# Gate and branch projections of a hybrid block: from weights on the stationary side with 256 tokens moving, to token tiles on the stationary side with 512 weight columns moving

## The chip, the cores and the metric

The kernel runs on one core of one Trainium2 chip. The metric is the device time of one execution in microseconds (us). TensorE (PE) does the matrix products, VectorE (DVE) and ScalarE (ACT) the elementwise work, GpSimd (POOL) mostly issues small transfers, and SyncE (SP) issues the weight loads. Engines run independently and wait for one another on semaphores; a tile in a rotating pool can be written again only when its last reader is done.

## The reference

One layer, one sequence of 256 tokens, width D = 2048, all in fp32:

```
mod = silu(c) @ w_ada + b_ada ;  sh1, sc1, g1, sh2, sc2, g2 = split(mod, 6)
h = rms_norm(x, mix_norm_pre) * (1 + sc1) + sh1
ya, yb, yc = hgrn2(h @ w_in ...), dilated_attention(...), conv_module(...)
gates = sigmoid(h @ w_gate + b_gate).reshape(B, S, 3, D)
merged = gates[0] * (ya @ w_a_out) + gates[1] * (yb @ w_b_out) + gates[2] * (yc @ w_c_out)
x = x + g1 * rms_norm(merged @ w_o, mix_norm_post)
h = rms_norm(x, mlp_norm_pre) * (1 + sc2) + sh2
x = x + g2 * rms_norm(square(relu(h @ w_up)) @ w_down, mlp_norm_post)
```

The change concerns `gates`, the three branch projections (2048 of their input columns together) and `merged`, which the product with `w_o` reads.

## The kernel before

Every product of two fp32 matrices is made of three products of split values. A weight tile `raw` of 512 KB is loaded by SP, ACT casts it to its high part `hi` (L126), DVE subtracts to get the low part `lo` (L127), and PE adds up weight-hi by activation-hi, weight-hi by activation-lo and weight-lo by activation-hi.

The work is one list of **jobs**, written out in Python in the order in which the weights are to be used. A job is one 512 KB load, its split, its matmuls, and what has to be done when its output tile is complete. `run` (L176) walks the list: up to five loads are issued ahead of the job at hand and up to four splits are made ahead; there are six `raw`, six `hi` and six `lo` tiles. So SP's queue holds the weight loads in list order, and each engine sees the instructions in the order in which the walk wrote them.

The jobs the change touches are the 96 **gate jobs** (12 gate tiles `g` of 512 output columns, for four column groups n and three branches b, eight jobs each) and the 32 **projection jobs** (four groups n, eight jobs: four for branch 0, one for branch 1, three for branch 2). The first 32 gate jobs stand by themselves. The others are woven with the projection jobs, the first `w_o` jobs and 96 **ada jobs** (names `wada`, `adap`, `adat`): such a job loads 512 KB too, but has no matmul: DVE multiplies the tile by the broadcast condition and sums along it (L297). In the stretch of gates there is nearly one ada job for each gate job. After every eighth ada job of the first 32, POOL writes 2 KB to a scratch in DRAM in elements of 4 bytes (L841, `np_scratch`) and reads it back repeated to all partitions (L843).

Both gate and projection jobs call `mm_a`: for each of two 128-row slices of the weight tile and each of four groups of 128 weight columns, the weights are the stationary operand and the 256 tokens move, 24 matmuls with 256 columns each. Outputs stand with weight columns on partitions, tokens along the tile. That makes the gate's bias one number per partition, which ACT adds while it reads the gate's sums out of PSUM (L824, four instructions of 256 elements). The finished `merged[n]` is already in the layout that the `w_o` product needs, so it is only split (L879 on ACT, L880 on DVE). The `w_o` jobs already use `mm_b`, in which a tile of 128 tokens is the stationary operand and 512 weight columns move, 12 matmuls for a job; so do the jobs of the first input projections (names L264 to L266; L252 to L254 belong to `mm_a`).

Of the kernel before, what the change touches and what calls it, by code (L numbers as in the profile page):

```python
# [19 lines left out]
P = 128  # L20
# [25 lines left out]
VEC = {}  # L46
_o = 0
for _n, _w in (("c", 16), ("lb", 8), ("b1", 32), ("b2", 32), ("bg1", 16), ("bg2", 16),
               ("n1", 16), ("n2", 16), ("np1", 16), ("np2", 16), ("bg", 48), ("cw", 186), ("cb", 6), ("lng", 6), ("lnb", 6),
               ("hw", 1)):  # L50
    VEC[_n] = (_o, _o + _w)
    _o += _w
# [4 lines left out]
def hybrid_block(ctx: ExitStack, tc: tile.TileContext, a, out, dbg=None):  # L57
# [182 lines left out]
    def mm_a(ps, h, l, na, ah, al, first, last, tk=None):  # L240

        t0, t1 = (0, S) if tk is None else (tk * P, (tk + 1) * P)
        bk = ps if isinstance(ps, list) else [ps[:, 0, :], ps[:, 1, :]]
        head = first and tk != 1
        for i in range(na):
            f, e = head and i == 0, last and i == na - 1
            x, y = ah[i][:, t0:t1], al[i][:, t0:t1]
            for j in range(h.shape[2] // P):
                o = bk[j // 2][:, (j % 2) * S + t0:(j % 2) * S + t1]
                w = slice(j * P, (j + 1) * P)  # L250
                b0, b1 = j % 2 == 0, j % 2 == 1
                nc.tensor.matmul(o, h[:, i, w], x, start=f and b0, stop=False, skip_group_check=True)  # L252
                nc.tensor.matmul(o, h[:, i, w], y, start=False, stop=False, skip_group_check=True)  # L253
                nc.tensor.matmul(o, l[:, i, w], x, start=False, stop=e and b1, skip_group_check=True)  # L254
# [13 lines left out]
    def ps_unit():  # L268
        return psg.tile([P, 2, 512], F32, tag="g", name=nm("g"))
# [120 lines left out]
    def h_hi(kt):  # L390
        return hT[kt // 2][:, 0, kt % 2, :]

    def h_lo(kt):
        return hT[kt // 2][:, 1, kt % 2, :]
# [417 lines left out]
    st_ln = []  # L812

    def gate_job(b, n, ch):
        def fn(h, l):
            if ch == 0:
                pst["gt"] = ps_unit()
            kts = [2 * ch, 2 * ch + 1]
            mm_a(pst["gt"], h, l, 2, [h_hi(k) for k in kts], [h_lo(k) for k in kts], ch == 0, ch == 7)
            if ch == 7:  # L820
                gates[b, n] = s4([P, 4, S])
                for j in range(4):
                    c = b * 16 + n * 4 + j
                    g = nc.scalar.activation(gates[b, n][:, j, :], pst["gt"][:, j // 2, (j % 2) * S:(j % 2 + 1) * S],  # L824
                                             AF.Sigmoid, bias=V("bg")[:, c:c + 1])
                if (b, n) == (2, 3):
                    with tc.issue_after(g.ins):
                        st_ln.append(nc.scalar.preload_act_table_set("natural_log_exp_and_others"))
        return Job(a["wg"][(b * 4 + n) * 8 + ch], [P, 2, 512], fn, budget=B_G)

# [21 lines left out]
    def act_of(ki):  # L852
# [3 lines left out]
            return ybT[0]  # L856
        return ycT[ki - 5]

    def proj_job(n, ki):
        b = 0 if ki < 4 else (1 if ki == 4 else 2)  # L860
        first, last = ki in (0, 4, 5), ki in (3, 4, 7)

        def fn(h, l):
            if first:
                pst["pj"] = ps_unit()
            t = act_of(ki)
            mm_a(pst["pj"], h, l, 2, [t[:, 0, 0, :], t[:, 0, 1, :]], [t[:, 1, 0, :], t[:, 1, 1, :]], first, last)
            if last:
                g = gates[b, n]
                gv = g.rearrange("p a b -> p (a b)")  # L870
                nc.vector.tensor_mul(gv, pst["pj"].rearrange("p a b -> p (a b)"), gv)
                if b == 0:
                    merged[n] = g
                else:
                    nc.vector.tensor_add(merged[n], merged[n], g)
                if b == 2:
                    mh = s4([P, 4, S], F32R)
                    ml = s4([P, 4, S], F32R)
                    nc.scalar.copy(mh, merged[n])  # L879
                    nc.vector.tensor_sub(ml, merged[n], mh.bitcast(F32))  # L880
                    mhl[n] = (mh, ml)
                    dump(f"mg{n}", merged[n].rearrange("p a b -> p (a b)"))
        return Job(a["wp"][n * 8 + ki], [P, 2, 512], fn, budget=B_P)

# [309 lines left out]
def layout(inputs):  # L1194
# [16 lines left out]
    for k in range(3):  # L1211
# [13 lines left out]
    ad = cat(pair(sc1, sh1) + [g1] + pair(sc2, sh2) + [g2], 1)  # L1225
    a["wada"] = np.ascontiguousarray(ad.T.reshape(96, P, 2, 1024).transpose(0, 2, 1, 3)).reshape(192, P, 1024)
    a["wada0"] = _chunks(cat([sc1[:, :256], sh1[:, :256]], 1))
    b = i["b_ada"][0].reshape(6, D)
    two = lambda u, v: np.ascontiguousarray(np.stack([_cols(u, 16), _cols(v, 16)], 2)).reshape(P, 32)
    cw = i["conv_w"][0].T.reshape(6, P, 31).transpose(1, 0, 2).reshape(P, 186)  # L1230
    a["vec"] = np.ascontiguousarray(cat([
        _cols(i["c"], 16), _cols(i["hgrn_lb_logits"], 8), two(b[1], b[0]), two(b[4], b[3]), _cols(b[2], 16),
        _cols(b[5], 16), _cols(i["mix_norm_pre"], 16), _cols(i["mlp_norm_pre"], 16), _cols(i["mix_norm_post"], 16),
        _cols(i["mlp_norm_post"], 16), _cols(i["b_gate"], 48), cw,
        _cols(i["conv_b"], 6), _cols(i["conv_ln_g"], 6), _cols(i["conv_ln_b"], 6), _cols(i["hgrn_norm_w"], 1)], 1))
    return a

# [13 lines left out]
```

## Time and profile before

| quantity | value |
|---|---|
| time, median of 3 runs | 1692.66 us (1688.83 to 1697.15) |
| time of the profiled execution | 1685.17 us |
| its span, first to last instruction | 1683.1 us |
| mean granted clock of TensorE | 0.995 of full speed |
| PE busy | 1631.5 us, 97% of the span |
| DVE busy | 1163.8 us, 69% |
| ACT busy | 748.1 us, 44% |
| POOL busy | 48.7 us, 3% |
| DMA, mean over the span | 240 GB/s |

The profile is of one execution; 2.1 us of its time lie outside the span. Busy times are shares of the whole span, over stages that differ much: the gate and projection jobs lie between about 310 and 850 us, and what holds there has to be read from views of that stretch. A matmul's busy time overlaps with that of the next, so the distance from one start to the next, and not the duration of a row, is what a matmul takes in a stream.

### The profile page before, as it was taken

The numbers are of one execution on the slowest core, as the hardware profiler recorded it, in microseconds if no ns is written. First come the engines' busy times: TensorE is split into PE (matmuls) and PEld (weight loads), VectorE is DVE, ScalarE is ACT, GpSimd is POOL, SyncE is SP. The second block draws the span as 40 slices with busy tenths as digits, with TensorE's granted clock in tenths as the row PEclk, the third lists the DMA queues.
The fourth block names the chain that finished last, engine by engine and source line by source line (L and its number), as shares of the span: only waits on it lengthen the run. The fifth ranks groups of instructions, "written<-read, shape, count | busy, mean of one in ns | idle before, by whom it ended". The sixth has DMA issues, their size and how long they took to land.

```text
span 1683.1 us, 27691 instructions
## 1 busy us (share of the span) xinstructions
PE 1631.5 (97%) x11142; PEld 1507.7 (90%) x11142; DVE 1163.8 (69%) x1549; ACT 748.1 (44%) x891; POOL 48.7 (3%) x74
## 2 busy tenths in 40 slices
PE   5999999989999999999999899999999999999997
PEld 3899999877999999999988799999999988888886
DVE  5899979638898986898896665454545745444444
ACT  3644443334453453444444654434444644333333
POOL 0000000110000000000000300000000000000000
PEclk9999999999999999999999999999999999999999
DMA  8999985663344899999898477778777876666662
GB/s 280 347 325 348 320 316 185 188 188 113 116 151 130 262 313 280 367 372 351 299 335 311 133 243 240 203 248 206 245 213 251 222 235 208 190 196 192 195 192 76
DMA packets 112114, 403.33 MB, mean 240 GB/s; under 512 B 13157, under 2 KB 13553, under 8 KB 111985
## 3 DMA queue, kind: packets, MB, share of 16 engines
q1 hardware_dynamic: 107280, 388.24, 70.4%
q0 software_dynamic: 4416, 13.18, 2.4%
q8 instruction: 87, 1.43, 0.4%
q14 instruction: 43, 0.34, 0.1%
q10 hardware_dynamic: 288, 0.13, 0.0%
HBM read 397.28 MB, written 6.59 MB: 240 GB/s over the span
## 4 chain that ended last, share of the span: by engine, by line
PE 80%; DMA 10%; DVE 6%; ACT 2%; issue 2%; DVEq 0%; POOL 0%; SPq 0%; ACTq 0%; POOLq 0%
PE g L254 14%; PE g L252 14%; PE g L253 14%; DMA raw<-wada 5%; PE g L1126 5%; PE g L1127 5%; PE g L1128 5%; PE g L266 4%; PE g L265 4%; PE g L264 4%; DVE lo L127 3%; DMA raw<-wg 3%; PE m L1126 2%; PE m L1127 2%; PE m L1128 2%
## 5 line engine op out<-in xcount | busy, mean ns | idle before, releaser
L126 ACT CAST hi<-raw 128x1024 fp32r<-128x1024 f32 x538 | 563.9, 1050 | 800.0 <-PE g L253 281.8
L127 DVE TENSOR_TENSOR lo<-raw,hi 128x1024 fp32r<-128x1024 f32 x534 | 647.0, 1223 | 263.3 <-ACT hi L126 261.3
L254 PE MATMUL g<-s,lo 128*128 128x256 f32 x2560 | 727.1, 284 | 8.1 <-DVE lo L127 8.1
L252 PE MATMUL g<-s,hi 128*128 128x256 f32 x2560 | 726.6, 284 | 0.7 <-ACT hi L126 0.7
L253 PE MATMUL g<-s,hi 128*128 128x256 f32 x2560 | 725.3, 283 | 0.0
L254 PEld LDWEIGHTS g<-s,lo 128*128 128x128 f32 x2560 | 491.8, 192 | 10.1 <-DVE lo L127 9.9
L252 PEld LDWEIGHTS g<-s,hi 128*128 128x128 f32 x2560 | 492.0, 192 | 1.0 <-ACT hi L126 0.9
L253 PEld LDWEIGHTS g<-s,hi 128*128 128x128 f32 x2560 | 492.0, 192 | 0.0
L297 DVE SCALAR_TENSOR_TENSOR raw<-raw,s 128x1024 f32<-128x1024 f32 x184 | 224.6, 1222 | 165.2 <-DMA raw<-wada 165.0
L1126 PE MATMUL g<-hi,s 128*128 128x512 f32 x384 | 149.4, 389 | 0.0
L1127 PE MATMUL g<-lo,s 128*128 128x512 f32 x384 | 149.4, 389 | 0.0
L1128 PE MATMUL g<-hi,s 128*128 128x512 f32 x384 | 149.4, 389 | 0.0
L266 PE MATMUL g<-hi,s 128*128 128x512 f32 (+1 forms) x344 | 132.5, 385 | 2.1 <-DVE s L940 2.1
L265 PE MATMUL g<-lo,s 128*128 128x512 f32 (+1 forms) x344 | 131.7, 383 | 0.3 <-DVE lo L127 0.3
L264 PE MATMUL g<-hi,s 128*128 128x512 f32 (+1 forms) x344 | 131.8, 383 | 0.0
L1128 PEld LDWEIGHTS g<-hi,s 128*128 128x128 f32 x384 | 72.1, 188 | 15.0
L1126 PEld LDWEIGHTS g<-hi,s 128*128 128x128 f32 x384 | 72.1, 188 | 14.9
L1127 PEld LDWEIGHTS g<-lo,s 128*128 128x128 f32 x384 | 72.1, 188 | 14.8
L266 PEld LDWEIGHTS g<-hi,s 128*128 128x128 f32 x344 | 65.0, 189 | 16.3 <-DVE s L940 3.3
L450 DVE SCALAR_TENSOR_TENSOR s<-s,vec,s 128x256 f32<-128x256 f32 x180 | 77.9, 480 | 0.0
L264 PEld LDWEIGHTS g<-hi,s 128*128 128x128 f32 x344 | 64.9, 189 | 14.0 <-issue 1.6
L265 PEld LDWEIGHTS g<-lo,s 128*128 128x128 f32 x344 | 64.8, 189 | 13.8 <-issue 1.0
(215 smaller groups left out, 1067.5 us busy)
## 6 DMA issues: line engine op xcount, KB each, us to landing
raw<-wada SPq DMA_DIRECT2D x192, 512.0 KB, 5.4
raw<-wu SPq DMA_DIRECT2D x128, 512.0 KB, 4.7
raw<-wd SPq DMA_DIRECT2D x128, 512.0 KB, 4.3
raw<-wg SPq DMA_DIRECT2D x96, 512.0 KB, 5.2
raw<-w SPq DMA_DIRECT2D x80, 512.0 KB, 5.1
raw<-wv SPq DMA_DIRECT2D x44, 512.0 KB, 3.8
raw<-wp SPq DMA_DIRECT2D x32, 512.0 KB, 5.7
raw<-wo SPq DMA_DIRECT2D x32, 512.0 KB, 5.2
```

What stands on the lines that cost most here:

```text
L126: nc.scalar.copy(h, raw)
L127: (eng or nc.vector).tensor_sub(l, raw, h.bitcast(F32))
L252: nc.tensor.matmul(o, h[:, i, w], x, start=f and b0, stop=False, skip_group_check=True)
L253: nc.tensor.matmul(o, h[:, i, w], y, start=False, stop=False, skip_group_check=True)
L254: nc.tensor.matmul(o, l[:, i, w], x, start=False, stop=e and b1, skip_group_check=True)
L264: nc.tensor.matmul(o, ah[i][:, tk], h[:, i, :], start=f, stop=False)
L265: nc.tensor.matmul(o, ah[i][:, tk], l[:, i, :], start=False, stop=False)
L266: nc.tensor.matmul(o, al[i][:, tk], h[:, i, :], start=False, stop=e)
L297: nc.vector.scalar_tensor_tensor(raw, raw, 1.0, cbc[q % 2], op0=ALU.mult, op1=ALU.mult, accum_out=st["p"][:, q:q + 1])
L1126: nc.tensor.matmul(o, uh[:, kt % 4, tk], h[:, 0, w], start=kt == 0, stop=False)
L1127: nc.tensor.matmul(o, uh[:, kt % 4, tk], l[:, 0, w], start=False, stop=False)
L1128: nc.tensor.matmul(o, ul[:, kt % 4, tk], h[:, 0, w], start=False, stop=kt == 63)
```

## The change

Gate and projection jobs call `mm_b`: the token tile is stationary, 512 weight columns move, 12 matmuls of 512 columns for each job instead of 24 of 256. Their outputs have tokens on partitions, `[128, 2, 512]`. The job list, and with it the order of the weight loads, stays as it was. Three things follow from the other layout:

- The gate's bias lies along the tile now. For each of the 12 gates POOL loads a tile of 128 x 512 (256 KB) that repeats one row of 2 KB, when the gate's first job is written out; DVE adds it to the sums in PSUM (L826, 128 x 1024), and ACT applies one sigmoid to the sum (L827).
- `merged[n]` has to be turned before the `w_o` product: `merge_gen` makes, for each n, eight transposes on PE of 128 x 128, four into each of two PSUM banks (L871), two copies on ACT out of PSUM (L875, 512 elements each) and two subtractions on DVE (L876). They are steps of a side chain that the walk takes one by one after jobs; the first four steps are empty (`MERGE_WAIT`).
- The vector of per-partition constants loses the 48 columns of the gate bias (218.5 KB becomes 194.5 KB).

```
 def gate_job(b, n, ch):
     def fn(h, l):
         if ch == 0:
             pst["gt"] = ps_unit()
+            pst["gb"] = s2([P, 512])
+            b0 = a["bgate"][0:1, b * D + n * 512:b * D + (n + 1) * 512]
+            nc.gpsimd.dma_start(pst["gb"], bass.AP(tensor=b0.tensor, offset=b0.offset, ap=[[0, P], [1, 512]]))
         kts = [2 * ch, 2 * ch + 1]
-        mm_a(pst["gt"], h, l, 2, [h_hi(k) for k in kts], [h_lo(k) for k in kts], ch == 0, ch == 7)
+        mm_b(pst["gt"], h, l, 2, [h_hi(k) for k in kts], [h_lo(k) for k in kts], ch == 0, ch == 7)
         if ch == 7:
-            gates[b, n] = s4([P, 4, S])
-            for j in range(4):
-                c = b * 16 + n * 4 + j
-                g = nc.scalar.activation(gates[b, n][:, j, :], pst["gt"][:, j // 2, (j % 2) * S:(j % 2 + 1) * S],
-                                         AF.Sigmoid, bias=V("bg")[:, c:c + 1])
+            g = gates[b, n] = s4([P, 2, 512])
+            nc.vector.tensor_add(g, pst["gt"], pst["gb"][:, None, :].to_broadcast([P, 2, 512]))
+            e = nc.scalar.activation(g, g, AF.Sigmoid)
...
+def merge_gen(n):
+    for _ in range(MERGE_WAIT):
+        yield 0.0
+    mh, ml = s4([P, 4, S], F32R), s4([P, 4, S], F32R)
+    mhl[n] = (mh, ml)
+    for q in range(2):
+        ps = bank()
+        for j in range(2):
+            for t in range(2):
+                nc.tensor.transpose(ps[:, j * S + t * P:j * S + (t + 1) * P],
+                                    merged[n][:, t, (2 * q + j) * P:(2 * q + j + 1) * P], ident)
+        psv = ps.rearrange("p (a b) -> p a b", a=2)
+        k = slice(2 * q, 2 * q + 2)
+        nc.scalar.copy(mh[:, k, :], psv)
+        nc.vector.tensor_sub(ml[:, k, :], psv, mh[:, k, :].bitcast(F32))
+        yield 0.6
...
 def proj_job(n, ki):
...
-        mm_a(pst["pj"], h, l, 2, [t[:, 0, 0, :], t[:, 0, 1, :]], [t[:, 1, 0, :], t[:, 1, 1, :]], first, last)
+        mm_b(pst["pj"], h, l, 2, [t[:, 0, 0, :], t[:, 0, 1, :]], [t[:, 1, 0, :], t[:, 1, 1, :]], first, last)
         if last:
             g = gates[b, n]
-            gv = g.rearrange("p a b -> p (a b)")
-            nc.vector.tensor_mul(gv, pst["pj"].rearrange("p a b -> p (a b)"), gv)
+            nc.vector.tensor_mul(g, pst["pj"], g)
             if b == 0:
                 merged[n] = g
             else:
                 nc.vector.tensor_add(merged[n], merged[n], g)
             if b == 2:
-                mh = s4([P, 4, S], F32R)
-                ml = s4([P, 4, S], F32R)
-                nc.scalar.copy(mh, merged[n])
-                nc.vector.tensor_sub(ml, merged[n], mh.bitcast(F32))
-                mhl[n] = (mh, ml)
+                add_side(-1, merge_gen(n))
```

The first place is the end of a gate, on the engines that read its sums. Before, ACT does it. These are ACT's rows around the end of the eleventh gate (`g_7725`): `hi_7887` belongs to that gate's last job, and the casts behind it to the next jobs.

```order
L126 CAST hi_7887<-raw_7882 128x1024
L126 CAST hi_7924<-raw_7915 128x1024
L126 CAST hi_7958<-raw_7952 128x1024
L126 CAST hi_7996<-raw_7991 128x1024
L126 CAST hi_8030<-raw_8025 128x1024
L126 CAST hi_8060<-raw_8028 128x1024
L824 ACTIVATE s_1133_7986<-g_7725,vec 128x256 x4
L126 CAST hi_8093<-raw_8065 128x1024
```

After, DVE does it. These are DVE's rows around the same gate's end (`g_6681` there; `lo_6786` belongs to its last job, `lo_6811` and `lo_6833` to the two jobs behind it).

```order
L127 TENSOR_TENSOR lo_6786<-raw_6780,hi_6785 128x1024
L297 SCALAR_TENSOR_TENSOR raw_6783,adap_6828<-raw_6783,s_30_192 128x1024
L127 TENSOR_TENSOR lo_6811<-raw_6801,hi_6810 128x1024
L826 TENSOR_TENSOR s_1146_6848<-g_6681,s_1115_6682 128x1024
L297 SCALAR_TENSOR_TENSOR raw_6808,adap_6828<-raw_6808,s_28_181 128x1024
L127 TENSOR_TENSOR lo_6833<-raw_6826,hi_6832 128x1024
L297 SCALAR_TENSOR_TENSOR raw_6830,adap_6828<-raw_6830,s_30_192 128x1024
L127 TENSOR_TENSOR lo_6857<-raw_6851,hi_6856 128x1024
```

The reader of the gate's sums moved from behind five casts of later jobs on ACT to behind one subtraction of a later job on DVE.

The second place is POOL's queue in the woven stretch. Before, it holds only the write and the read of the scratch there, four times.

```order
L674 DMA s_612_3948<-bias_rows 128x256 x3
L841 DMA np_scratch<-adat_6069 128x4x1
L843 DMA s_883_6074<-np_scratch 128x512
L841 DMA np_scratch<-adat_6347 128x4x1
L843 DMA s_920_6352<-np_scratch 128x512
```

After, POOL's queue from the last rows of the attention bias (L646, L674) to the second scratch pair:

```order
L646 DMA bias_rows<-bias_scratch 128x384 x4
L821 DMA s_677_4342<-bgate 128x512
L674 DMA s_515_3499<-bias_rows 128x256
L821 DMA s_712_4579<-bgate 128x512
L674 DMA s_546_3635<-bias_rows 128x256 x3
L674 DMA s_581_3804<-bias_rows 128x256 x3
L674 DMA s_612_3948<-bias_rows 128x256 x3
L821 DMA s_762_4849<-bgate 128x512
L821 DMA s_796_5087<-bgate 128x512
L821 DMA s_837_5341<-bgate 128x512
L843 DMA np_scratch<-adat_5589 128x4x1
L845 DMA s_888_5594<-np_scratch 128x512
```

Two of the bias loads stand ahead of reads that the attention waits for, three follow in the first gates, and the other seven come during and behind the scratch pairs.

The third place is PE, where the transposes of the first merge stand inside a gate job (`g_6502`, its weights `hi_6459` and `lo_6460`).

```order
L266 MATMUL g_6502<-hi_6459,s_95_538 128x512
L871 MATMUL m_6482<-ident,s_706_4555 128x128 x4
L871 MATMUL m_6489<-ident,s_706_4555 128x128 x4
L264 MATMUL g_6502<-hi_6459,s_95_538 128x512
L265 MATMUL g_6502<-lo_6460,s_95_538 128x512
```

Nothing of the kind stood there before; L264 to L266 are the matmuls of the other form.

## Rows read from the trace of the kernel before

**Rows 1.** Chain that ended last, by engine (page).

```profile
PE 80%; DMA 10%; DVE 6%; ACT 2%; issue 2%; DVEq 0%; POOL 0%; SPq 0%; ACTq 0%; POOLq 0%
```

**Rows 2.** Timeline of PE, a stream of 256-column matmuls: start, us, engine, line.

```profile
699.75 0.28 PE L253 MATMUL g<-s,hi 128*128 128x256 f32 x1
...
700.59 0.28 PE L254 MATMUL g<-s,lo 128*128 128x256 f32 x1
```

**Rows 3.** Timeline of PE, a stream of 512-column matmuls in the MLP.

```profile
1400.00 0.39 PE L1128 MATMUL m<-hi,s 128*128 128x512 f32 x1
...
1401.36 0.39 PE L1128 MATMUL g<-hi,s 128*128 128x512 f32 x1
```

**Rows 4.** Busy time in three windows: us, PE, PEld, DVE, ACT, POOL, clock, DMA, GB/s.

```profile
440.00:560.00 120.00, 119.57 (x1015) 118.97 (x1014) 110.44 (x201) 48.90 (x90) 0.00 (x0) 1.00 0.45 139
560.00:700.00 140.00, 134.05 (x1088) 132.16 (x1088) 112.43 (x170) 63.92 (x87) 5.21 (x8) 1.00 0.97 311
700.00:850.00 150.00, 150.00 (x1246) 149.70 (x1245) 132.06 (x164) 64.97 (x70) 2.85 (x4) 1.00 0.93 339
```

**Rows 5.** Waits, 560 to 700 us.

```profile
ACT hi L126 <- DMA raw<-wg: 49.8, 25, 6.7
...
PE g L254 <- DVE lo L127: 4.0, 4, 2.3
```

**Rows 6.** Timeline of POOL's queue, 575 to 690 us, first and last of four writes.

```profile
579.43 0.78 POOL L841 DMA_DIRECT2D np_scratch<-adat  x1 [170.90 <-DVE adat L839]
...
660.64 0.76 POOL L841 DMA_DIRECT2D np_scratch<-adat  x1 [16.48 <-DVE adat L839]
```

**Rows 7.** Windows at and between those writes; the last number is GB/s.

```profile
579.00:590.00 11.00, 11.00 (x82) 10.56 (x81) 9.62 (x17) 4.44 (x7) 1.17 (x2) 1.00 0.81 165
...
660.00:672.00 12.00, 12.00 (x102) 12.00 (x101) 7.45 (x11) 2.30 (x4) 0.89 (x2) 1.00 0.96 210
...
740.00:780.00 40.00, 40.00 (x335) 40.00 (x335) 35.25 (x48) 17.99 (x22) 0.34 (x1) 1.00 1.01 398
```

**Rows 8.** DMA issues: KB each, median us from issue to landing.

```profile
s<-np_scratch POOLq DMA_DIRECT2D x8, 256.0 KB, 6.5
...
np_scratch<-adat POOLq DMA_DIRECT2D x8, 2.0 KB, 10.6
```

**Rows 9.** Windows of L127 alone (DVE): splits finished since 415 us.

```profile
415.00:575.00 160.00, 50.48 (x42) 0.00 (x0) 1.00 0.50 160
...
415.00:672.00 257.00, 83.87 (x69) 0.00 (x0) 1.00 0.68 208
```

**Rows 10.** Windows of L254 alone (PE): eight for each job.

```profile
415.00:575.00 160.00, 84.47 (x297) 56.81 (x297) 1.00 0.50 160
...
415.00:672.00 257.00, 154.67 (x543) 104.10 (x544) 1.00 0.68 208
...
415.00:775.00 360.00, 233.33 (x820) 157.16 (x821) 1.00 0.76 255
```

**Rows 11.** Groups by line and shape: busy us, mean ns of one, idle before.

```profile
L127 DVE TENSOR_TENSOR lo<-raw,hi 128x1024 fp32r<-128x1024 f32 x534 | 647.0, 1223 | 263.3 <-ACT hi L126 261.3
...
L297 DVE SCALAR_TENSOR_TENSOR raw<-raw,s 128x1024 f32<-128x1024 f32 x184 | 224.6, 1222 | 165.2 <-DMA raw<-wada 165.0
...
L824 ACT ACTIVATE s<-g,vec 128x256 f32<-128x256 f32 x48 | 18.7, 476 | 2.0 <-PE g L254 2.0
...
L1059 ACT ACTIVATE s<-s 128x1024 f32<-128x1024 f32 x15 | 15.9, 1060 | 0.4
...
L871 DVE TENSOR_TENSOR s<-g,s 128x1024 f32<-128x1024 f32 x12 | 14.7, 1221 | 1.3 <-PE g L254 1.3
```

**Rows 12.** Chain of waits, four 128 x 128 matmuls with the identity: start, us.

```profile
385.96 0.44 PE m L704 x4
```

**Rows 13.** Waits, 318 to 370 us, the attention's bias.

```profile
DVE s L690 <- DMA s<-bias_rows: 7.0, 1, 7.0
```

**Rows 14.** Window 300 to 380 us; clock 0.98 (third from the end).

```profile
300.00:380.00 80.00, 73.65 (x364) 58.75 (x364) 40.86 (x49) 30.75 (x38) 11.65 (x22) 0.98 0.61 190
```

More of the change, by code (lines that the diff above doesn't have):

```diff
@@ L48 @@
 for _n, _w in (("c", 16), ("lb", 8), ("b1", 32), ("b2", 32), ("bg1", 16), ("bg2", 16),
-               ("n1", 16), ("n2", 16), ("np1", 16), ("np2", 16), ("bg", 48), ("cw", 186), ("cb", 6), ("lng", 6), ("lnb", 6),
+               ("n1", 16), ("n2", 16), ("np1", 16), ("np2", 16), ("cw", 186), ("cb", 6), ("lng", 6), ("lnb", 6),
                ("hw", 1)):
@@ L817, in fn @@
                 pst["gt"] = ps_unit()
+                pst["gb"] = s2([P, 512])
+                b0 = a["bgate"][0:1, b * D + n * 512:b * D + (n + 1) * 512]
+                nc.gpsimd.dma_start(pst["gb"], bass.AP(tensor=b0.tensor, offset=b0.offset, ap=[[0, P], [1, 512]]))
             kts = [2 * ch, 2 * ch + 1]
-            mm_a(pst["gt"], h, l, 2, [h_hi(k) for k in kts], [h_lo(k) for k in kts], ch == 0, ch == 7)
+            mm_b(pst["gt"], h, l, 2, [h_hi(k) for k in kts], [h_lo(k) for k in kts], ch == 0, ch == 7)
             if ch == 7:
-                gates[b, n] = s4([P, 4, S])
-                for j in range(4):
-                    c = b * 16 + n * 4 + j
-                    g = nc.scalar.activation(gates[b, n][:, j, :], pst["gt"][:, j // 2, (j % 2) * S:(j % 2 + 1) * S],
-                                             AF.Sigmoid, bias=V("bg")[:, c:c + 1])
+                g = gates[b, n] = s4([P, 2, 512])
+                nc.vector.tensor_add(g, pst["gt"], pst["gb"][:, None, :].to_broadcast([P, 2, 512]))
+                e = nc.scalar.activation(g, g, AF.Sigmoid)
                 if (b, n) == (2, 3):
-                    with tc.issue_after(g.ins):
+                    with tc.issue_after(e.ins):
                         st_ln.append(nc.scalar.preload_act_table_set("natural_log_exp_and_others"))
@@ L857, in act_of @@
         return ycT[ki - 5]
+    def merge_gen(n):
[14 more added lines that the diff above has]
+            yield 0.6
+    MERGE_WAIT = 4
     def proj_job(n, ki):
@@ L1227, in layout @@
     a["wada0"] = _chunks(cat([sc1[:, :256], sh1[:, :256]], 1))
+    a["bgate"] = np.ascontiguousarray(i["b_gate"])
     b = i["b_ada"][0].reshape(6, D)
@@ L1233, in layout @@
         _cols(b[5], 16), _cols(i["mix_norm_pre"], 16), _cols(i["mlp_norm_pre"], 16), _cols(i["mix_norm_post"], 16),
-        _cols(i["mlp_norm_post"], 16), _cols(i["b_gate"], 48), cw,
+        _cols(i["mlp_norm_post"], 16), cw,
         _cols(i["conv_b"], 6), _cols(i["conv_ln_g"], 6), _cols(i["conv_ln_b"], 6), _cols(i["hgrn_norm_w"], 1)], 1))
```

## The prediction

> **What bounds the kernel now.** I read the chain that ended last first: four fifths of it are TensorE, a tenth is transfers, DVE follows with 6% [rows 1]. So matmul time counts, but not everywhere, and the windows say where. From 440 to 560 us PE is busy for 119.57 of 120 us while the DMA engines stand at 0.45; from 560 to 700 us PE loses 6 of 140 us and DMA is at 0.97; from 700 to 850 us PE is full again and DMA at 0.93 [rows 4]. PE bounds the gates' first part, the loads the middle, and the last part holds both close together. The waits of the middle confirm it: ACT's casts wait 49.8 us for weight loads, and PE itself only 4.0 us, 2.3 at the longest, for the low parts [rows 5]. PE was shielded by what had been split ahead. Since 415 us, 42 splits were finished by 575 us against 297 / 8 = 37.1 jobs multiplied; by 672 us it was 69 against 67.9 [rows 9, 10]: five jobs of lead shrank to one.
>
> What takes the lead is on POOL's queue. Four times, from 579.43 to 660.64 us, 2 KB are written in 4-byte elements [rows 6], and each time the rate falls from the 398 GB/s that loads can reach to 165 (first) or 210 (last) for 11 or 12 us [rows 7]; 11 x (1 - 165 / 398) = 6.4 and 12 x (1 - 210 / 398) = 5.7 us of loading are lost there, some 24 in all four. The write lands after 10.6 us [rows 8].
>
> **The change, part by part.** Durations are those of the profiled execution (1685.17 us, 7.49 below the median 1692.66), and the sum is made against it; the forecast adds the 7.49 back.
>
> *Matmuls.* Starts of 256-column matmuls lie 0.84 / 7 = 0.120 us apart [rows 2], those of 512 columns 1.36 / 6 = 0.2267 us [rows 3]. A job goes from 24 x 0.120 = 2.88 to 12 x 0.2267 = 2.72 us; 128 jobs win 128 x 0.16 = **20.5 us** where PE binds. The trace shows the long form in this kernel with weights moving, in the MLP, so I carry the pitch over without a margin.
>
> The Trainium skill, page "TensorE: Matmul & The Clock Gate", section "Back-to-back issue gap", gives an isolated gap of N / 2.4 + 2.5 ns, 109.2 for 256 and 215.8 for 512 columns. By it a job would win only 0.03 us and all jobs some 4, by estimate, and the sum below would come out near +15, a slower kernel; that is the last rival's case. The trace disagrees on the short form (0.120 where the page has 0.109), and the measurement decides.
>
> *Transposes.* Eight for each of four merges, 32 in all, had no counterpart before. Four matmuls of that shape with the identity take 0.44 us on the chain [rows 12], so 32 x 0.11 = **+3.5 us**. The first three merges stand between gate jobs and the last among the output jobs; I take all of it as PE time. Where PE waits for loads they are free, so the bounds are 1.8 (half of them) and 3.5.
>
> *Elementwise work.* ACT loses 48 x 0.476 = 22.8 us and gets 12 x 1.06 = 12.7 [rows 11] and half-size copies in place of full ones. DVE gets 12 additions at the 1.22 us of its 1,024-element product out of PSUM [rows 11], 14.7 us; the merge's subtractions come to the same elements as before. Sums alone cost nothing: ACT is at 64 of 140 us and DVE at 112 of 140 [rows 4]. What they cost by standing in the queue comes below. The smaller vector saves 24 KB at the start, below 0.1 us at the rates of [rows 7].
>
> *Loads that bind.* Nearly every gate job has an ada load with it, so a pair moves 1.05 MB; in 2.88 us that asks for 364 GB/s, in 2.72 us for 385, where 398 is the best window [rows 7]. DVE needs two instructions of 1.22 us for the pair, 2.45 us [rows 11]. Three engines come within 10% of each other. From 575 to 672 us PE ran (543 - 297) / 8 = 31 jobs at the pace of loads; they win nothing, 31 x 0.16 = 5.0 us to give back. From 672 to 775 us (820 - 543) / 8 = 35 more ran while the lead was built up again [rows 10]; with loads needed at 385 GB/s it builds up hardly at all. Bounds: 5.0 if only the first lot is lost, 66 x 0.16 = 10.6 if both are. Because 385 is within 4% of 398, I take **+8.5**.
>
> *Bias loads.* A tile of 256 KB takes 0.68 us of the engines at 385 GB/s, whatever its latency (the like read of the scratch lands in 6.5 us [rows 8]). Five of twelve come before the loads bind; seven stand during and behind the scratch pairs, where they push weight loads back: 7 x 0.68 = 4.8 us at most, nothing if the lead has recovered by then. I take **+4**, near the upper end, as most stand in the stretch of [rows 7]. They are issued when the gate's first job is written out, eight jobs ahead of the addition, over 20 us against 6.5 of landing, so no addition waits for one.
>
> *Attention.* Two of them go ahead of reads of the attention's bias rows, a chain at whose end DVE already waits 7.0 us [rows 13] and PE behind it. Nothing to 2 x 0.68 = 1.4 us; **+1**, since that chain sits on the path.
>
> *Ends of gates.* Before, ACT reads the sums behind five later casts, so nothing waits. After, DVE's addition stands behind one later subtraction for the last six gates, and DVE can't pass it before PE finishes the gate. Then follow 1.22 for the addition, 1.22 for the ada product, 1.22 for the next subtraction, 3.7 us in all, while PE has one job, 2.72 us: it waits 1.0 us. I count three gates in the order where the ada product stands in between; in the others two instructions, 2.4 us, are covered by that job. So 3.0 us at most for PE itself, nothing where PE waits for loads already: **+2**. What else is queued behind the addition is ada products and subtractions, which set weight buffers free; that is the second rival. The transposes stand 17 to 23 matmuls (3.9 us and more) behind the projection whose product and sum DVE makes in 2.4 us, so PE doesn't wait for them.
>
> Sum: -20.5 + 3.5 + 8.5 + 4 + 1 + 2 = **-1.5**, that is 1683.7 against the profiled 1685.17, or 1691.2 on the median's scale.
>
> **Rivals.**
>
> *Loads keep up (faster).* The window from 740 us reaches 398 GB/s [rows 7], and the last part before had PE full at 339 GB/s on average [rows 4]. If the loads' price falls to its lower bound 5.0 less the 2 us that a quicker entry into the stretch could leave, and bias loads and gate ends are covered, -20.5 + 3.5 + 3 + 1 = -13: 1679.7 on the median's scale. Against it: five jobs of lead were gone by 672 us.
>
> *Gate ends starve the loads (slower).* One mechanism, DVE held at the addition. The ada product and the subtraction ahead of it take 2.45 of the 2.72 us of PE's last job, so DVE stands for 0.27 us and then works 1.22 on the sums: the ada product behind, and the buffer that it frees, are 1.5 us late. With six buffers and loads of 5 us in flight, each such delay is a hole in the load stream where that binds. Seven gates lie there: 7 x 1.5 = 10 us, and 3 x 1.0 on PE, 13 in place of 2: 11 more on the sum, 1702.2. It decides once nearly the whole of each hold reaches the loads.
>
> *PE waits longer and its clock falls.* In the window from 300 to 380 us, where PE stood still for the attention's bias, the granted clock is 0.98 [rows 14]: 80 x 0.02 = 1.6 us for one fall to 1.2 GHz. With waits of 5 us in place of 2.3 [rows 5], four falls add 6.5: 1697.7.
>
> *The change doesn't bring the short job.* If the long form's pitch in this stretch is 0.240 and not 0.2267, nothing is won by the matmuls and the sum is +19: 1711.7. Only the early gates, where nothing else binds, tell it.
>
> **How the numbers follow.** About 0.5%, 8.5 us, is what a measurement of this kernel can tell from no change: below 1684.2 is faster, above 1701.1 slower. The sum as it stands: 0.42, all of it within. Loads keep up: 0.29, of which 0.26 falls below 1684.2 and 0.03 within. Gate ends: 0.16, close above the border, 0.13 slower and 0.03 within. The clock: 0.09, of which 0.05 within and, with the gate ends partly beside it, 0.04 slower. No short job: 0.04, slower. That makes 0.26 faster, 0.53 the same and 0.21 slower. The range leaves out the lower third of the first rival, the upper part of the second and the last: 1678 to 1706.
>
> **What would show it.** A pitch of 0.227 us in gate jobs; PE full up to 570 us and those jobs 5 us earlier; then PE's waits from 575 us on above 10 us in total, for low parts, with DMA at 0.97 or more; the rate falling four times again. Right on the ends of gates: waits of 1 us on PE after the addition in three of them. Wrong altogether if PE stays full from 560 to 700 us, or if the additions wait for their bias tiles.

## The result and the profile after

The changed kernel is slower: 1712.99 us against 1691.32 before, each the median of four runs; the ratio is 1.0121, with an interval of 1.0092 to 1.0150. The forecast was 1691 with a range of 1678 to 1706, so the time lies above the range. The profiled execution took 1715.8 us. Its mean granted clock is 0.983, where it was 0.995.

The three windows that answer to [rows 4], of the changed kernel (us, PE, PEld, DVE, ACT, POOL, clock, DMA share, GB/s):

```profile
440.00:560.00 120.00, 119.22 (x681) 102.70 (x680) 108.41 (x195) 48.91 (x84) 0.00 (x0) 1.00 0.40 121
560.00:700.00 140.00, 116.06 (x470) 91.31 (x468) 106.63 (x164) 49.27 (x57) 6.80 (x11) 0.93 0.91 264
700.00:850.00 150.00, 143.76 (x621) 116.67 (x621) 127.66 (x162) 64.14 (x64) 3.98 (x7) 0.98 0.93 339
```

PE is full up to 560 us, as before. Then it loses 24 of 140 us, where it lost 6, and the rate of the loads is 264 GB/s and not 311. The clock, 1.00 throughout before, is 0.93.

The waits from 560 to 700 us, to be held against [rows 5]:

```profile
ACT hi L126 <- DMA raw<-wg: 78.8, 27, 9.4
...
PE g L264 <- ACT hi L126: 19.1, 5, 6.9
...
PE g L265 <- DVE lo L127: 3.4, 5, 0.8
```

PE waits now mostly for high parts, which come one cast behind a load: next to nothing is ahead of it any more. The longest wait is 6.9 us, three times that of before. What a wait of this length does stands in PE's timeline just behind it:

```profile
617.03 0.80 PE L264 MATMUL g<-hi,s 128*128 128x512 f32 x1 [6.89 <-ACT hi L126]
617.62 0.63 PE L265 MATMUL g<-lo,s 128*128 128x512 f32 x1
618.05 0.63 PE L266 MATMUL g<-hi,s 128*128 128x512 f32 x1
618.48 0.63 PE L264 MATMUL g<-hi,s 128*128 128x512 f32 x1
```

The starts lie 0.43 us apart, at 1.2 GHz: the granted clock is 0.50 from 617 to 619.5 us. Where PE runs undisturbed, the pitch is the forecast one; between these two starts lie nine intervals, (751.84 - 749.80) / 9 = 0.2267 us:

```profile
749.80 0.39 PE L264 MATMUL g<-hi,s 128*128 128x512 f32 x1
...
751.84 0.39 PE L264 MATMUL g<-hi,s 128*128 128x512 f32 x1
```

Windows of 20 us show that the loss comes in strokes:

```profile
580.00:600.00 20.00, 19.32 (x86) 16.12 (x87) 19.04 (x37) 6.90 (x9) 0.77 (x1) 1.00 0.94 277
600.00:620.00 20.00, 8.94 (x30) 6.23 (x29) 14.65 (x21) 11.73 (x18) 1.08 (x2) 0.84 0.79 260
...
640.00:660.00 20.00, 18.65 (x67) 14.60 (x68) 15.01 (x21) 7.76 (x8) 1.63 (x3) 0.83 0.97 371
660.00:680.00 20.00, 13.50 (x49) 10.29 (x48) 9.12 (x12) 3.15 (x3) 1.07 (x2) 0.83 0.99 218
...
700.00:720.00 20.00, 15.06 (x48) 10.59 (x48) 10.88 (x13) 6.37 (x7) 2.12 (x4) 0.83 0.96 338
```

POOL's queue says where they come from. These are the first and the last of the four scratch writes, with what follows the first (compare [rows 6]):

```profile
593.09 0.77 POOL L843 DMA_DIRECT2D np_scratch<-adat  x1 [179.30 <-DVE adat L841]
603.10 0.54 POOL L845 DMA_DIRECT2D s<-np_scratch  x1 [9.23 <-DMA np_scratch<-adat]
603.95 0.54 POOL L821 DMA_DIRECT2D s<-bgate  x1 [0.32 <-issue]
...
690.86 0.76 POOL L843 DMA_DIRECT2D np_scratch<-adat  x1 [18.45 <-DVE adat L841]
```

In the 11 us from the first and from the last write on, the core's transfers move 177 and 202 GB/s:

```profile
593.00:604.00 11.00, 9.17 (x41) 7.27 (x39) 10.21 (x18) 2.83 (x3) 1.36 (x3) 1.00 0.88 177
...
690.00:701.00 11.00, 10.08 (x45) 8.01 (x43) 7.46 (x13) 2.11 (x2) 0.76 (x1) 1.00 1.10 202
```

Each write is followed by one of PE's losses. The four now lie 98 us from first to last, before 81. And PE comes to them with next to nothing in hand. To see this, count the splits finished since the first gate's (L127) against the matmuls of L264, four for each job, up to 575 us; the kernel before stands first (its first gate split starts at 416.6 us, and the next split ends behind 575), then the changed kernel's splits, then its matmuls:

```profile
416.00:574.20 158.20, 48.78 (x40) 0.00 (x0) 1.00 0.50 160
```

```profile
420.00:575.00 155.00, 46.22 (x38) 0.00 (x0) 1.00 0.46 138
```

```profile
430.50:575.00 144.50, 59.35 (x149) 28.04 (x149) 1.00 0.44 133
```

38 splits against 149 / 4 = 37.25 jobs: a lead of 0.75 jobs, which is nothing beyond the job in hand. Before, it is 40 against the 37.1 jobs of [rows 10], a lead of 2.9; the 42 of [rows 9] take in the last split of the input projections and one not yet finished. Counted in the same way at each kernel's first scratch write (579 and 593 us), the lead is 4.4 jobs before and 1.25 after.

### The profile page after: what moved, and what is told of

It reads as the page before. It is cut to its first block, busy times and chain, and to the rows that moved or that the text cites. A ratio compares the mean times of both kernels' runs of the same rounds, so it can differ in the third digit from the quotient of the medians.

```text
span 1714.0 us, 24671 instructions
## 1 busy us (share of the span) xinstructions
PE 1634.8 (95%) x9638; PEld 1437.8 (84%) x9638; DVE 1176.5 (69%) x1565; ACT 741.8 (43%) x859; POOL 55.1 (3%) x86
## 4 chain that ended last, share of the span: by engine, by line
PE 72%; DMA 12%; DVE 9%; issue 3%; ACT 3%; POOL 0%; DVEq 0%; ACTq 0%; SPq 0%; POOLq 0%
PE g L254 10%; PE g L252 10%; PE g L253 10%; DMA raw<-wg 6%; PE g L266 5%; PE g L264 5%; PE g L265 5%; PE g L1145 5%; PE g L1144 5%; PE g L1143 5%; DVE lo L127 4%; DMA raw<-wada 3%; DVE raw L297 2%; PE m L1145 2%; PE m L1144 2%
## 5 line engine op out<-in xcount | busy, mean ns | idle before, releaser
L127 DVE TENSOR_TENSOR lo<-raw,hi 128x1024 fp32r<-128x1024 f32 x534 | 645.5, 1221 | 281.8 <-ACT hi L126 280.6
L254 PE MATMUL g<-s,lo 128*128 128x256 f32 x1536 | 435.5, 284 | 2.8 <-DVE lo L127 2.8
L253 PE MATMUL g<-s,hi 128*128 128x256 f32 x1536 | 434.7, 283 | 0.0
L252 PE MATMUL g<-s,hi 128*128 128x256 f32 x1536 | 434.6, 283 | 0.0
L264 PE MATMUL g<-hi,s 128*128 128x512 f32 (+1 forms) x856 | 339.9, 397 | 22.1 <-ACT hi L126 22.1
L265 PE MATMUL g<-lo,s 128*128 128x512 f32 (+1 forms) x856 | 339.5, 397 | 7.1 <-DVE lo L127 7.0
L266 PE MATMUL g<-hi,s 128*128 128x512 f32 (+1 forms) x856 | 338.4, 395 | 2.9 <-DVE s L957 2.9
L254 PEld LDWEIGHTS g<-s,lo 128*128 128x128 f32 x1536 | 294.8, 192 | 4.0 <-DVE lo L127 4.0
L252 PEld LDWEIGHTS g<-s,hi 128*128 128x128 f32 x1536 | 294.8, 192 | 0.0
L253 PEld LDWEIGHTS g<-s,hi 128*128 128x128 f32 x1536 | 294.8, 192 | 0.0
L264 PEld LDWEIGHTS g<-hi,s 128*128 128x128 f32 x856 | 164.8, 193 | 59.6 <-ACT hi L126 25.5
L265 PEld LDWEIGHTS g<-lo,s 128*128 128x128 f32 x856 | 164.7, 192 | 45.6 <-DVE lo L127 12.0
L266 PEld LDWEIGHTS g<-hi,s 128*128 128x128 f32 x856 | 165.0, 193 | 38.0 <-DVE s L957 3.8
L1144 PEld LDWEIGHTS g<-lo,s 128*128 128x128 f32 x384 | 72.1, 188 | 15.1
L1145 PEld LDWEIGHTS g<-hi,s 128*128 128x128 f32 x384 | 72.1, 188 | 14.8
L1143 PEld LDWEIGHTS g<-hi,s 128*128 128x128 f32 x384 | 72.0, 188 | 14.9
L450 DVE SCALAR_TENSOR_TENSOR s<-s,vec,s 128x256 f32<-128x256 f32 x180 | 77.9, 475 | 0.0
```

The source lines that it names most:

```text
L127: (eng or nc.vector).tensor_sub(l, raw, h.bitcast(F32))
L264: nc.tensor.matmul(o, ah[i][:, tk], h[:, i, :], start=f, stop=False)
L265: nc.tensor.matmul(o, ah[i][:, tk], l[:, i, :], start=False, stop=False)
L266: nc.tensor.matmul(o, al[i][:, tk], h[:, i, :], start=False, stop=e)
L1143: nc.tensor.matmul(o, uh[:, kt % 4, tk], h[:, 0, w], start=kt == 0, stop=False)
L1144: nc.tensor.matmul(o, uh[:, kt % 4, tk], l[:, 0, w], start=False, stop=False)
```

## The experiments

Three theories were set against each other first. **DVE:** its twelve additions use up the lead. **Loads:** the bias tiles on POOL's queue hold up attention and weight loads. **Shape:** PE merely reaches the loads sooner. Later runs add **scratch** (the holes that the four 2 KB writes tear into the load stream are what PE waits for), **lead** (DVE lags before the loads bind, so PE arrives with nothing ahead) and **bytes** (weight loads and bias tiles ask for more than can be moved, holes or not). All ratios are against the kernel before on the same chip, whose median was 1681 to 1684 us there; the times in us that are worked out from them are ratios times that. Traces are of one execution for each kernel. Where a kernel leaves out part of the computation, its expectation says so.

### One edit after another, with the scratch as it was

**Form alone**, `e4_shape_only`:

```
 (kernel before)
-mm_a(pst["gt"], ...)      mm_a(pst["pj"], ...)
+mm_b(pst["gt"], ...)      mm_b(pst["pj"], ...)
```

> The kernel before with nothing but the matmul form exchanged in gate and projection jobs; outputs stand in the other layout and are treated as before (bias as if per partition, merged tile not transposed), so the output is another. DVE and loads theories: -20.5 + 5 to 8 = -15 to -12, 1676 to 1680 us. Shape theory: no gain, within 5 us of the kernel before.

**Neither loads nor additions**, `e3_neither`, which has the transposes on top of the form:

```
 (changed kernel)
-pst["gb"] = s2([P, 512]) and its load
-nc.vector.tensor_add(g, pst["gt"], ...)
-e = nc.scalar.activation(g, g, AF.Sigmoid)
+e = nc.scalar.activation(g, pst["gt"], AF.Sigmoid)
```

> Leaves out the gate's bias, its loads and its additions: ACT takes the sigmoid out of PSUM. DVE and loads theories both: -20.5 for the matmuls, +3.5 for the transposes, +5 to +8 for loads that bind, so 1678 to 1684 us. Shape theory: no gain over the kernel before, 1688 us or more.

**Loads without additions**, `e2_no_add` (the tiles are loaded again, the additions stay out):

> Leaves out the gate's bias: the bias tiles are still loaded, but nothing reads them, and ACT takes the sigmoid of the sums straight out of PSUM, so that DVE does nothing at a gate's end. DVE theory: the lead of 12 to 14 us at 560 us comes back and with it some 15 us, 1693 to 1699 (the loads' own cost stays). Loads theory: little changes, 1706 to 1713. Shape theory: 1705 to 1713.

**Additions without loads**, `e1_no_loads`:

```
 (changed kernel, no bias tiles)
-nc.vector.tensor_add(g, pst["gt"], pst["gb"][:, None, :].to_broadcast([P, 2, 512]))
+nc.vector.tensor_add(g, pst["gt"], ones[:, None, 0:1].to_broadcast([P, 2, 512]))
```

> Leaves out the gate's bias: no bias tiles are loaded, and DVE's addition at each gate's end reads a constant column instead; everything else as in the changed kernel. DVE theory (the twelve additions on DVE use up the lead of the splits before the loads bind): the additions are still there, so most of the loss stays, 1700 to 1707 us, and PE's lead at 560 us is still 2 to 4 us. Loads theory (the bias tiles on POOL's queue hold up the attention and crowd the weight loads): the loss goes, about 1690 us. Shape theory (PE merely reaches the loads sooner, no edit beside it matters): 1705 to 1713.

| kernel | median us | ratio to before | interval |
|---|---|---|---|
| form alone | 1690.02 | 1.0047 | 1.0028 to 1.0065 |
| and transposes (`e3_neither`) | 1691.31 | 1.0064 | 1.0038 to 1.0090 |
| and loads (`e2_no_add`) | 1697.27 | 1.0087 | 1.0062 to 1.0112 |
| and additions: the changed kernel | 1712.99 | 1.0121 | 1.0092 to 1.0150 |
| additions without loads (`e1_no_loads`) | 1706.87 | 1.0141 | 1.0108 to 1.0174 |

The form alone is slower by 8 us (0.0047 x 1683), and 12 us of gain were expected of it by my sum; none of the three theories had a loss of more than 5. That is by far the largest miss; the other steps are 3 us for the transposes, 4 for the loads, 6 to 13 for the additions, and neighbouring intervals overlap. The loads theory falls: without bias tiles the kernel is no faster. (The last but one row was measured against a median before of 1691.32, the others against 1683.08; the ratios are comparable, the medians are not.) The expected times stand on a scale on which the kernel before takes 1691 us; carried over to it by their ratios, the four runs come to 1699, 1702, 1706 and 1715 us in the order of their expectations. The DVE theory holds for a part (6 us come back without the additions, where it had 15); the shape theory was nearest.

The profile of the form alone shows the changed kernel's pattern with nothing but the form: the windows from 600 and from 680 us,

```profile
600.00:620.00 20.00, 16.18 (x63) 12.32 (x61) 14.86 (x26) 10.15 (x16) 0.54 (x1) 0.91 0.84 289
...
680.00:700.00 20.00, 14.98 (x56) 11.52 (x55) 11.56 (x16) 4.20 (x4) 0.54 (x1) 0.83 0.90 248
```

with a falling clock, and the lead at 575 us, splits first (the next one ends behind 575), then L264:

```profile
419.50:573.90 154.40, 46.38 (x38) 0.00 (x0) 0.97 0.44 141
...
435.00:575.00 140.00, 58.32 (x147) 27.64 (x147) 1.00 0.45 142
```

38 - 147 / 4 = 1.25 jobs, against 2.9 before and 0.75 in the changed kernel; at its own first scratch write (592 us) it is 3.0, against 4.4 and 1.25. PE runs ahead of a DVE that works no faster, so the form takes a part of the lead, and the other edits, the additions on DVE among them, take more.

### Without the holes

**Rows in the changed kernel**, `e5_rows_after`, and **rows in the kernel before**, `e6_rows_before`, with the same edit (it takes in the four later writes of this kind, from about 1050 us on, as well):

```
+def np_gen(G, i, d, t):            # a step of the side chain
+    yield 0.0
+    ps = bank()
+    nc.tensor.transpose(ps[:4, :P], t, ident)
+    row = s2([4, P])
+    nc.scalar.copy(row, ps[:4, :P])
+    nc.gpsimd.dma_start(d[4 * i:4 * i + 4, :], row)
...
-nc.gpsimd.dma_start(d[4 * i:4 * i + 4, :].rearrange("j p -> p j"), t)
+add_side(-1, np_gen(G, i, d, t))
```

> The changed kernel, with the 2 KB to the scratch written as four rows of 512 bytes (PE turns the 128 x 4 tile, ACT copies it) instead of in 4-byte elements. Scratch theory (the four holes of about 6 us in the load stream are what PE waits for): PE's waits between 560 and 720 us fall from 42 to under 20 us, and the time comes down by 18 to 24 us, to between -3 and +5 us of the kernel before. Bytes theory (weight loads and bias tiles ask for more than the engines can move, holes or not): under 10 us come back. Lead theory (DVE lags before the loads bind, so PE arrives with nothing ahead): some 10 us come back, as the shorter holes still find no lead.

> The kernel before with the same row-wise write. Scratch theory: PE lost about 7 us between 560 and 700 us there, so -4 to -7 us against the kernel before. Bytes theory: within 2 us. Lead theory: -4 to -7 as well, since the lead of 14 us covered the rest.

The changed kernel gets 1683.84 us, ratio 0.9995 (0.9975 to 1.0014): some 21 us come back (1.0121 - 0.9995 = 0.0126). The kernel before wins little, 1679.21, ratio 0.9975 (0.9950 to 1.0000). So the same writes cost the one kernel some 4 us and the other 21. This is what the scratch theory had given; the bytes theory, by which under 10 us come back, falls. The landing of the write in the changed kernel with rows (KB each, median us):

```profile
np_scratch<-s POOLq DMA_DIRECT2D x8, 2.0 KB, 3.7
```

In place of 10.6 us [rows 8] it lands in 3.7, both medians of all eight writes; the four between 560 and 720 us take 5.0 in place of 10.3. The holes are gone: from the first and from the last of these writes on, the rate is 290 and 366 GB/s, where it was 177 and 202.

```profile
601.00:612.00 11.00, 5.99 (x25) 4.08 (x23) 11.00 (x19) 8.97 (x17) 1.61 (x3) 1.00 0.84 290
...
671.00:682.00 11.00, 11.00 (x50) 9.06 (x49) 10.05 (x13) 4.53 (x6) 2.65 (x5) 1.00 0.97 366
```

The rate from 570 to 700 us rises from 267 to 337 GB/s; the changed kernel first, then the one with rows:

```profile
570.00:700.00 130.00, 106.14 (x425) 83.30 (x423) 96.63 (x145) 47.06 (x55) 6.80 (x11) 0.92 0.92 267
```

```profile
570.00:700.00 130.00, 119.42 (x498) 94.69 (x497) 114.60 (x169) 60.21 (x71) 7.47 (x14) 0.96 0.92 337
```

**Form and rows**, `e10_shape_rows` (the edit of the form alone and that of the rows, in the kernel before):

> The matmul form alone, as in the run of that name, together with row-wise scratch writes; the output stands in the other layout and is treated as before, so it is another. If the shorter job pays wherever loads don't hold PE up (scratch theory): -4 for the rows, -20.5 for the matmuls, +5 that DVE takes back between 430 and 570 us, +3 where PE runs at the loads' pace, so -19 to -13 us against the kernel before. If the form never pays, whatever the loads do (a cost of the long form itself): -4 or above.

1667.48 us, ratio 0.9910 (0.9879 to 0.9941), 15 us faster than before and 11 faster than before with rows (0.9975 - 0.9910 = 0.0065). The form pays as soon as nothing else holds the loads up; there is no cost in the long matmul itself. PE is busy for 127 of 130 us there, at full clock:

```profile
570.00:700.00 130.00, 127.28 (x562) 103.70 (x561) 114.86 (x169) 65.95 (x92) 4.31 (x8) 1.00 0.93 344
```

All these kernels walk the same job list, so the stretch can be cut by jobs instead of by time. These are the 26 jobs from the start of the 39th gate or projection job, about where the first scratch write falls, to the start of the 65th: 208 matmuls of L254 in the kernel before and in the kernel before with rows, 104 of L264 in the form alone, the changed kernel, the changed kernel with rows, and form and rows, in this order.

```profile
580.72:660.86 80.14, 59.15 (x208) 39.92 (x209) 1.00 0.97 298
```

```profile
576.75:654.63 77.88, 59.03 (x208) 39.92 (x209) 1.00 0.97 348
```

```profile
582.15:674.69 92.54, 42.53 (x104) 20.55 (x104) 0.94 0.92 287
```

```profile
579.05:685.37 106.32, 43.84 (x104) 21.20 (x104) 0.90 0.92 273
```

```profile
580.24:664.40 84.16, 41.70 (x104) 19.87 (x104) 0.98 0.93 338
```

```profile
582.81:659.14 76.33, 40.97 (x104) 19.52 (x104) 1.00 0.94 345
```

With the holes the form costs 12 us here, 92.5 - 80.1, and without them it wins 2, 77.9 - 76.3. The whole change costs 26 us here with the holes and 6 without. Or, the other way round: the holes cost 2 us here in the kernel before, 16 with the form alone and 22 in the changed kernel. So nearly all that the rows give back in the new form lies in these 26 jobs.

### What takes the rest back

With rows the form wins 15 us and the whole changed kernel nothing. Three runs add one of the other edits each.

**Additions**, `e13_form_add` (form and rows, and at each gate's end):

```
-four nc.scalar.activation(..., bias=V("bg")[:, c:c + 1])
+nc.vector.tensor_add(gv, pst["gt"], ones[:, None, 0:1].to_broadcast([P, 2, 512]))
+g = nc.scalar.activation(gv, gv, AF.Sigmoid)
```

> Form and row-wise writes alone (-15 us against the kernel before), and DVE's addition with one sigmoid at each gate's end, with a constant column in place of the bias; outputs stand in the other layout, so the output is another. If the additions hold DVE, and with it the loads: 8 to 12 of the 15 us are gone, -7 to -3. If they only cost PE 1 us at some gates' ends: -13 to -11.

**Bias loads**, `e14_form_loads` (form and rows, and the twelve loads of the change):

> Form and row-wise writes alone, and the twelve bias tiles loaded on POOL's queue, which nothing reads; the output is another, as before. If the tiles crowd the weight loads: up to 7 x 0.68 = 5 us are lost, -10. If they are covered now: within 2 us of -15.

**Transposes**, `e12_no_add_rows` (`e3_neither` with rows and `MERGE_WAIT = 8`):

> The changed kernel with row-wise writes and eight empty steps, without the bias (no tiles, no additions; ACT takes the sigmoid out of PSUM). It stands to the form alone as the transposes do: 3.5 us for 32 transposes and 2 to 3 for gaps ahead of them, so -10 to -8 us. If the transposes cost much more than their own time (a longer wait at the last merge): -6 or above.

| kernel | median us | ratio to before | interval |
|---|---|---|---|
| form and rows | 1667.48 | 0.9910 | 0.9879 to 0.9941 |
| with additions | 1671.70 | 0.9957 | 0.9934 to 0.9980 |
| with bias loads | 1670.37 | 0.9946 | 0.9928 to 0.9965 |
| with transposes | 1672.15 | 0.9950 | 0.9926 to 0.9974 |

Each takes some 6 to 8 us by its ratio, just about what the noise lets one see: the intervals overlap with one another and with that of form and rows, so which is the largest can't be told. Together they come to 21 us, more than the 12 to 14 us between form and rows and the whole kernel. The bias loads' 6 us here and 4 us with the holes lie about the 4.8 us of seven tiles; that the run with additions and no loads was no faster than the changed kernel doesn't fit them, and stays unexplained.

**A later merge**, `e11_rows_merge` (`e5_rows_after` with `MERGE_WAIT = 8`):

> The changed kernel with row-wise scratch writes and eight empty steps ahead of a merge instead of four, so that its transposes stand further behind the projection. If the two gaps of PE ahead of transposes (1.3 and 2.5 us with rows alone) come from DVE's product and sum standing late in its queue, both go: 3 to 4 us less than with rows alone, -5 to -3 us against the kernel before. If the output jobs wait for the merge instead, nothing or a loss.

1682.03 us, the median of ten executions (one took 5672.77 us, and no trace shows why), ratio 0.9982 (0.9958 to 1.0006): not to be told from the rows alone. In the changed kernel PE had waited ahead of transposes, from 850 to 890 us, for DVE's last addition:

```profile
PE m L871 <- DVE s L896: 3.8, 2, 3.2
```

With rows and four steps the longest such gap of PE was 2.1 us, and with eight it is 2.1 us too. So the time is inconclusive, and the gap that the steps were to close did not close.

### Other ways to spare DVE

**Low parts on POOL**, `e7_pool_lo`, and the same with rows, `e8_rows_pool`:

```
-return Job(a["wg"][...], [P, 2, 512], fn, budget=B_G)
+return Job(a["wg"][...], [P, 2, 512], fn, budget=B_G,
+           lo_eng=nc.gpsimd if 3 * n + b < 4 and ch in (1, 5) else None)
```

> The changed kernel, with the low parts of eight of the first 32 gate jobs made on POOL instead of DVE: 8 x 1.22 = 9.8 us less on DVE between 430 and 570 us. Lead theory: PE's lead at 560 us rises from 3 to 10 us or more, and 7 to 10 us of the loss come back (+10 to +14 us against the kernel before). Scratch and bytes theories: a lead only moves the wait, under 4 us come back.

> The changed kernel with both: row-wise scratch writes and eight low parts on POOL. Scratch and lead theories together: PE full from 430 to 800 us, so the matmuls' gain shows: -20.5 + 3.5 + 5 for the last merge + 2 to 5 for gate ends, -10 to -5 us against the kernel before. Bytes theory: at or above the kernel before.

1.0132 (1.0097 to 1.0167) and 0.9990 (0.9966 to 1.0014): nothing gained in either, where the lead theory had 7 to 10 us coming back in the first, and the second was expected 5 to 10 us below the kernel before. From 430 to 570 us PE is no longer full in `e7_pool_lo`,

```profile
430.00:570.00 140.00, 131.91 (x750) 113.73 (x750) 126.26 (x214) 59.46 (x99) 19.09 (x10) 0.97 0.41 128
```

and DVE's own instructions are slower there, L450 taking 563 ns (kernel before, same stretch: 479; changed kernel: 476):

```profile
L450 DVE SCALAR_TENSOR_TENSOR s<-s,vec,s 128x256 f32<-128x256 f32 x74 | 38.7, 563 | 0.0
```

```profile
L450 DVE SCALAR_TENSOR_TENSOR s<-s,vec,s 128x256 f32<-128x256 f32 x68 | 30.1, 479 | 0.0
```

So the whole time is no clean trial of the lead: whatever it gave, PE and DVE paid for beside it. The cut by jobs says more. At its first scratch write (598.6 us) `e7_pool_lo` has 43 splits finished against 155 / 4 = 38.75 jobs, a lead of 4.25, about that of the kernel before (4.4). It comes from a late PE and not from early splits: at 575 us there are 36 splits and 32 jobs, in the changed kernel 38 and 37.25. Here are the 26 jobs in `e7_pool_lo` and in `e8_rows_pool`:

```profile
596.12:686.23 90.11, 42.38 (x104) 20.11 (x104) 0.96 0.95 276
```

```profile
584.73:658.71 73.98, 40.79 (x104) 19.52 (x104) 1.00 0.92 327
```

In `e7_pool_lo` PE enters them 17 us later than in the changed kernel and leaves them at nearly the same time, so they take 90.1 us and not 106.3; with rows it is 74.0 in place of 84.2. With more lead the stretch is shorter, then, but with the holes PE had lost as much before it, and no time is won. And with the lead of the kernel before, the holes still cost 90.1 - 74.0 = 16 us here, where they cost that kernel 80.1 - 77.9 = 2. So the lead as it is counted here is not all that covers the holes; what else does, no run shows.

**Addition on POOL**, `e9_rows_act` (rows, `MERGE_WAIT = 8`), and **addition some jobs later on DVE**, `e17_late_add` (the same base):

```
 e9_rows_act                                     e17_late_add
+nc.scalar.copy(g, pst["gt"])                    +nc.scalar.copy(g, pst["gt"])
+nc.gpsimd.tensor_add(g, g, gb ...)              +add_side(-1, gate_gen(b, n, g, gb))
+e = nc.scalar.activation(g, g, AF.Sigmoid)      +  # 4 empty steps, addition on DVE, sigmoid
```

> The changed kernel with row-wise scratch writes, eight empty steps, and the gate's end taken off DVE: ACT copies the sums out of PSUM, POOL adds the bias, ACT takes the sigmoid. Lead theory (DVE's additions cost 6 to 13 us, as the runs without them showed): 6 to 10 us less than with rows and eight steps, so -14 to -8 us against the kernel before. Rival (POOL's addition slows DVE beside it, as the low parts on POOL did, and ACT waits for it): no gain, -5 to 0.

> The changed kernel with row-wise writes and eight empty steps, in which ACT copies a gate's sums out of PSUM and DVE adds the bias some jobs later, so that DVE is not held at the gate's end; the whole computation is there. If being held is the cost: -10 to -6 us. If DVE's time is the cost (12 x 1.22 us before and while the loads bind): no better than with the additions at the end, -4 to 0.

1.0086 (1.0052 to 1.0120) and 1.0029 (1.0007 to 1.0051), both worse than DVE's addition at the gate's end (0.9982 with the same eight steps), and above all that had been expected of them. In `e17_late_add` ACT is held in DVE's place,

```profile
ACT s L836 <- PE g L266: 11.4, 6, 4.0
```

in its queue with the casts (560 to 850 us), and in `e9_rows_act` for POOL's sums besides. That this is what made them slower is an argument and not shown; shown is that taking the addition off the gate's end, or off DVE, doesn't help by itself.

## Why the prediction was wrong

**Right.** The pitch and the gain of 0.16 us a job; PE full to 560 us; waits of PE above 10 us in total behind it (though mostly for high parts, not low ones, and with DMA at 0.91, not 0.97); a rate that falls four times. The transposes measured 3 to 7 us where 3.5 stood. The bias loads' +4 measured 4 and 6, but nothing where the additions stood beside them.

**Wrong: the term "loads that bind", +8.5, with bounds of 5.0 and 10.6.** I gave back what the faster jobs could not win in that stretch and took for granted that its length would stay. The form alone measured +8 where the term leaves -12, so the term was 28.5, nearly three times its upper bound. Without the holes the same form measured -11 against its own base, and then the term is 9.5: inside the bounds. So 19 of the missing 20 us belong to the holes: I had counted 24 us of loading lost in them, and the lead that covered them before, and still used no number for what happens when the lead is gone. The cut by jobs puts it in one place: the holes cost 2 us of the 26 jobs in the kernel before and 16 with the form alone (92.5 against 76.3), where the term gave back only what the faster jobs win. That the lead had covered a cost which I did not price without it fits the counts, 4.4, 3.0 and 1.25 jobs at the first write and 80, 93 and 106 us; but it is in part an argument, as `e7_pool_lo` loses 16 us to the holes with a lead of 4.25. The lead shrank because PE won some 4 us in the first 32 gate jobs (126.8 us with the form alone, 131.0 before) while DVE, at 110 of 120 us [rows 4], did its splits no sooner, and DVE's first additions came on top. I had these numbers and read DVE's share of 80% in the next window instead. I also took the lead for larger than it was: finished gate splits are 40 and 68 at the two times of [rows 9], so it went from three jobs to none, not from five to one.

**Half right: the rival of the clock.** It asked for waits of 5 us and four falls for 6.5 us. The longest came to 6.9, and four windows show 0.83 or 0.84; falls followed shorter waits too, one of 2.5 us at 702.6. These windows are short of the full clock by (0.16 + 3 x 0.17) x 20 = 13.4 us, which is the most that the clock took from PE directly, while PE's waits from 560 to 720 us add up to 28.8 us, where they were 6.0. That clock and waits feed each other is likely, since a slow PE frees buffers late, but no run separates them: below that bound, the clock's part stays open. **Loads keep up** did not come about: 264 GB/s from 560 to 700 us. It is what form and rows show, with 344 and 15 us of gain.

**Ends of gates: +2, measured 6 to 13.** The mechanism of the rival (DVE held, buffers late) was given 11 more. The waits of DVE for a gate's last matmul are short (2.2 us in all from 560 to 700); the additions' own time before the loads bind took lead as well (at the first scratch write 3.0 jobs in `e2_no_add`, 1.25 in the changed kernel), which the sum set at nothing because DVE was not full.

**Attention: +1.** The clock falls there without bias tiles too: the window from 360 us shows 0.86 with the form alone and 0.99 with loads and no additions.

```profile
360.00:380.00 20.00, 20.00 (x88) 15.12 (x86) 8.66 (x12) 7.66 (x11) 1.60 (x3) 0.86 0.38 116
```

```profile
360.00:380.00 20.00, 20.00 (x101) 15.32 (x100) 8.65 (x13) 9.01 (x13) 1.59 (x3) 0.99 0.50 157
```

Nothing there shows the bias loads' doing. But the start of the gates moves with it: their first matmul comes 3.4 us later than before in the changed kernel's trace, 7.7 with the form alone and 0.2 with loads and no additions. How much of a median that makes, one trace of each doesn't show. **The merge** was said to make PE wait for nothing; it waited 3.8 us, because DVE's product and addition stand behind ada products and a split of later jobs, which I had left out of the 2.4 us.

## What to carry to other kernels

A stretch that is bound by loads has a length of its own, and the work split ahead of it pays at least in part for its worst moments: before making the bound engine faster, price the stretch with that lead at zero, and count the lead in finished splits. If a small transfer halves the load rate, remove it first; the same change can be a loss of 8 us with it and a gain of 11 without. Here twelve additions on an engine at 90% came with a lead of 1.25 jobs in place of 3.0, though that engine was not full.

## What was not expected of the hardware

A 2 KB write in 4-byte elements takes 10.6 us and some 6 us of a core's loading with it; as four rows of 512 bytes it lands in 3.7 us (5.0 in the stretch of the loads), and the rate beside it stays at 290 GB/s and more. Elementwise work on POOL in the stretch of DVE's small instructions came with one kind of these lengthened from 479 to 563 ns, 74 x 0.084 = 6.2 us, while seven subtractions moved there saved 7 x 1.22 = 8.5; `e8_rows_pool` shows the same, 575 ns, where rows alone have 480.
